# Up projections of two gated feed-forward layers by seven block products, with the normalised x as operand

## The chip, the cores and the metric

The kernel runs on one core of a Trainium2 chip. The metric is the device time of one execution in microseconds. Before the change three runs took 2679.86 to 2680.95 us, median 2680.18. The engines are TensorE (PE, with its weight loads shown apart as PEld), VectorE (DVE), ScalarE (ACT), GpSimd (POOL) and SyncE (SP), which here issues all the transfers.

## The reference, cut to what matters

A two-layer encoder works on 1024 prompt tokens and 32 tokens of a running stream, 1056 columns (TT) in all, with 1024 channels. Layer 0 has a gated convolution mixer, layer 1 an attention with a forget gate; each is followed by a feed-forward part:

```python
def _rmsnorm(x, g):
    y = xf * lax.rsqrt(jnp.mean(xf * xf, axis=-1, keepdims=True) + EPS)
    return (y * g)

def _conv_ffn(h, ctx, w_up, conv_w, w_down):       # h = _rmsnorm(x, ffn_norm[l])
    up = h @ w_up                                  # 1024 -> 2 * 2816
    upc, new_ctx = _causal_dwconv(up, ctx, conv_w) # three taps over time
    g, v = jnp.split(upc, 2, axis=-1)
    return (jax.nn.silu(g) * v) @ w_down, new_ctx  # 2816 -> 1024

x = x + f                                          # f is the result of _conv_ffn
```

All of it is float32.

## The kernel before

**Layout.** Channels lie in partitions, tokens along the free axis. x is eight tiles x[m] of 128 x 1056. Weights come as units of 128 x 1024: eight blocks of 128 x 128 (k = 0 to 7) that give one tile of 128 output channels.

**Precision.** Each operand is split into a rounded part (h, a copy by ACT) and the rest (l, a subtraction by DVE); a product is the three matmuls h*h, h*l and l*h (`chain`, L154 to L156). `weights` (L117) loads a unit, and splits it (L131, L132).

**An up unit** (`unit`, L170) has three column chunks of 352 (`CH`), with 8 x 3 matmuls each. Its operand is the split of the raw x times the norm's gain (`normed`, `split`). The factor 1/rms of each token, `rs`, is multiplied in when DVE reads the result from PSUM (L189). The first two units of a phase (`fresh`) don't wait for it: ACT copies them out as they are, and `settle` multiplies them later.

**The norm.** While x[m] is completed by the last down projection, ACT squares it and POOL (for the last m DVE) adds the square to acc (`square_add`, L205 and L206). `rstd` (L208) sums acc over partitions by a matmul with ones (L217), then works on tiles of 128 x 352 that hold the same number in all partitions: square root, reciprocal, one correcting step (L218 to L223).

**The feed-forward part** (`ffn`, L362). For each of 22 tiles t there are two units, g from unit t and v from unit 22 + t. Each goes through `halo`, `tail` (POOL copies of four columns) and `conv` (one ACT and two DVE instructions over 1058 columns, L266 to L268), g then through silu (L381); v*g (L383) is split into acth and actl (L140, L141). `pipeline` collects acts in groups of 2, 4, 4, 4, 4, 4. When the next group has its first act, `down` multiplies a group's acts by its w_down tiles: for each m and chunk, 3 matmuls per act, then DVE adds the PSUM bank to x[m] in SBUF (L291). x stays in SBUF through the whole part.

**The end.** The last group of layer 1 goes through `finish` (L226): four chunks of 264 columns (`ENDS`), each with its eight m, the sum of squares, the final norm, and the output's transfer. The last group of layer 0 calls `done(m)` for each m: x[m] is split for the attention (gain is folded into weights there) and spilled to DRAM. The attention phase reads x back for its output projection.

**Order.** The code is written for a scheduler that gives every instruction its engine's queue position and all semaphores at build time. Instructions written earlier have priority; one whose inputs or buffers aren't ready is passed by later ones. Engines then execute their queues in order. A pool of n buffers makes a writer wait until a buffer's last reader is done. PSUM has banks `d` (3 x 512), `s` (2 x 1024) and `o` (1 x 512) in all phases.

## Time and profile before

| what | value |
|---|---|
| median of three runs | 2680.18 us |
| the profiled execution: time; its span | 2678.83 us; 2677.0 us |
| mixer; feed-forward 0; attention; feed-forward 1 (stretches of the span, rounded) | 0 to 390; 390 to 1166; 1166 to 1890; 1890 to 2677 us |
| PE busy in 400 to 1166 (766 us) | 762.05 us |
| PE busy in 1890 to 2677 (787 us) | 766.28 us |
| bytes moved | 150.92 MB, mean 56 GB/s |

The span goes from the first to the last instruction; the time of an execution is 1.8 us longer here. A busy share is an average over stages, so stages are read from tables by stretch. PE's matmuls are pipelined: one is shown as some 320 ns long while the next starts after about half of that, so the pace is read from counts in a full stretch, not from the duration of one. In rows of groups the columns are: line, engine, operation, output<-inputs, shapes, count | busy us, mean ns of one | idle time of the engine before them and what ended it.

### The profile page before, as it was taken

What the parts mean: (1) busy time and instruction counts of PE and PEld (TensorE: products, weight loads), DVE (VectorE), ACT (ScalarE), POOL (GpSimd) and SP (SyncE); (2) the same over time, 40 slices, a digit from 0 to 9 for tenths busy, and PEclk for the clock granted to TensorE, in tenths of its full rate; (3) what the DMA queues carried; (4) which work ended last, traced back from release to release, by engine and by line L of the source; (5) the groups of instructions that cost most, each with busy time, mean ns of one, the idle gap of its engine ahead of it and who ended that gap; (6) DMA issues with size and microseconds to landing.
All of it is one profiled execution on the core that took longest, in us unless ns stands there. A gap on an engine that the chain in (4) does not pass through costs nothing.

```text
span 2677.0 us, 39027 instructions
## 1 busy us (share of the span) xinstructions
PE 2584.2 (97%) x16152; PEld 2534.1 (95%) x16152; DVE 1569.1 (59%) x2610; ACT 894.4 (33%) x1440; POOL 186.4 (7%) x291
## 2 busy tenths in 40 slices
PE   8999999999999999988999999999899999999997
PEld 7999999999999999988888888899899999999997
DVE  7444446554545455466787777767755454545547
ACT  4111133221212122235666656643422121212214
POOL 3000020000000000030000000001100000000003
PEclk9999999999999999989999999999999999999999
DMA  3111111111111111221221212261111111111111
GB/s 113 48 48 44 44 51 40 48 48 43 45 48 48 48 40 48 72 84 49 58 57 47 60 55 56 58 219 57 42 40 48 48 40 48 48 48 42 46 62 68
DMA packets 64929, 150.92 MB, mean 56 GB/s; under 512 B 12528, under 2 KB 34544, under 8 KB 64752
## 3 DMA queue, kind: packets, MB, share of 16 engines
q1 hardware_dynamic: 64752, 148.43, 17.1%
q8 instruction: 127, 2.08, 0.3%
q14 instruction: 50, 0.41, 0.0%
HBM read 121.87 MB, written 26.53 MB: 55 GB/s over the span
## 4 chain that ended last, share of the span: by engine, by line
PE 86%; DVE 8%; ACT 3%; issue 2%; DMA 1%; SPq 0%; DVEq 0%; ACTq 0%; POOL 0%; POOLq 0%
PE pb_d L154 15%; PE pb_d L155 15%; PE pb_d L156 15%; PE pb_s L154 8%; PE pb_s L156 8%; PE pb_s L155 8%; PE pb_o L154 4%; PE pb_o L156 4%; PE pb_o L155 4%; PE pb_o L624 2%; PE pb_d L635 1%; DVE pt L639 1%; DVE prob L580 1%; DVE wl L132 1%; DVE xl L144 1%
## 5 line engine op out<-in xcount | busy, mean ns | idle before, releaser
L154 PE MATMUL pb_d<-xh,wh 128*128 128x352 f32 (+2 forms) x1920 | 629.0, 329 | 16.9 <-ACT xh L143 7.1
L155 PE MATMUL pb_d<-xl,wh 128*128 128x352 f32 (+2 forms) x1920 | 627.6, 327 | 7.2 <-DVE xl L144 7.2
L156 PE MATMUL pb_d<-xh,wl 128*128 128x352 f32 (+2 forms) x1920 | 625.9, 326 | 1.1 <-DVE wl L132 0.9
L131 ACT ACTIVATE wh<-wraw 128x1024 fp32r<-128x1024 f32 (+1 forms) x197 | 208.1, 1056 | 1044.3 <-PE pb_d L155 445.8
L154 PEld LDWEIGHTS pb_d<-xh,wh 128*128 128x128 f32 x1920 | 364.8, 190 | 22.3 <-DVE pt L639 7.5
L155 PEld LDWEIGHTS pb_d<-xl,wh 128*128 128x128 f32 x1920 | 366.4, 191 | 9.8 <-DVE xl L144 9.4
L156 PEld LDWEIGHTS pb_d<-xh,wl 128*128 128x128 f32 x1920 | 365.5, 190 | 2.7 <-DVE wl L132 2.4
L132 DVE TENSOR_TENSOR wl<-wraw,wh 128x1024 fp32r<-128x1024 f32 (+1 forms) x197 | 244.9, 1243 | 102.6 <-ACT wh L131 102.2
L154 PE MATMUL pb_s<-xh,wh 128*128 128x352 f32 x896 | 292.2, 326 | 4.7 <-DVE u L189 4.7
L156 PE MATMUL pb_s<-xh,wl 128*128 128x352 f32 x896 | 290.0, 324 | 0.7 <-DVE wl L132 0.7
L155 PE MATMUL pb_s<-xl,wh 128*128 128x352 f32 x896 | 289.5, 323 | 0.0
L154 PE MATMUL pb_d<-acth,wh 128*128 128x352 f32 (+1 forms) x640 | 204.3, 320 | 0.8 <-ACT acth L140 0.8
L155 PE MATMUL pb_d<-actl,wh 128*128 128x352 f32 (+1 forms) x640 | 204.2, 319 | 0.4 <-DVE actl L141 0.4
L156 PE MATMUL pb_d<-acth,wl 128*128 128x352 f32 (+1 forms) x640 | 204.2, 319 | 0.0
L291 DVE TENSOR_TENSOR x<-x,pb_d 128x352 f32<-128x352 f32 x216 | 111.3, 519 | 155.7 <-PE pb_d L156 153.8
L189 DVE TENSOR_TENSOR u<-pb_d,rstd 128x352 f32<-128x352 f32 (+2 forms) x180 | 73.1, 429 | 210.3 <-PE pb_d L156 210.2
L154 PEld LDWEIGHTS pb_s<-xh,wh 128*128 128x128 f32 x896 | 169.1, 189 | 5.1 <-issue 4.9
L156 PEld LDWEIGHTS pb_s<-xh,wl 128*128 128x128 f32 x896 | 169.2, 189 | 1.0 <-DVE wl L132 1.0
L155 PEld LDWEIGHTS pb_s<-xl,wh 128*128 128x128 f32 x896 | 169.9, 190 | 0.2
L154 PE MATMUL pb_o<-xh,wh 128*128 128x352 f32 x448 | 145.2, 324 | 0.0
L156 PE MATMUL pb_o<-xh,wl 128*128 128x352 f32 x448 | 144.6, 323 | 0.0
L155 PE MATMUL pb_o<-xl,wh 128*128 128x352 f32 x448 | 144.3, 322 | 0.0
(237 smaller groups left out, 4729.5 us busy)
## 6 DMA issues: line engine op xcount, KB each, us to landing
wraw<-in_w_up SPq DMA_DIRECT2D x88, 512.0 KB
wraw<-in_w_down SPq DMA_DIRECT2D x44, 512.0 KB
wraw<-in_w_in SPq DMA_DIRECT2D x23, 512.0 KB
wraw<-in_w_kq SPq DMA_DIRECT2D x16, 512.0 KB
xd<-x SPq DMA_DIRECT2D x8, 528.0 KB
x<-xd SPq DMA_DIRECT2D x8, 528.0 KB
out_o_y<-y SPq DMA_DIRECT2D x16, 264.0 KB
wraw<-in_w_out SPq DMA_DIRECT2D x8, 512.0 KB
```

The costliest lines, as they stand in the source:

```text
L131: nc.scalar.activation(h[:, i:j], raw[:, i:j], AF.Copy)
L132: nc.vector.tensor_sub(l[:, i:j], raw[:, i:j], h[:, i:j].bitcast(F32))
L144: nc.vector.scalar_tensor_tensor(l[:, d], src[:, p], gain, h[:, d].bitcast(F32), op0=OP.mult, op1=OP.subtract)
L154: nc.tensor.matmul(ps, wh, xh[:, c[0]:c[1]], start=(i == 0), stop=False)
L155: nc.tensor.matmul(ps, wh, xl[:, c[0]:c[1]], start=False, stop=False)
L156: nc.tensor.matmul(ps, wl, xh[:, c[0]:c[1]], start=False, stop=(i == n - 1))
L189: nc.vector.tensor_mul(dst[:, d], ps[:, p.start - c[0]:p.stop - c[0]], self.rs[:, p])
L291: nc.vector.tensor_add(x[m][:, c[0]:c[1]], x[m][:, c[0]:c[1]], ps[:, :c[1] - c[0]])
L580: nc.vector.tensor_tensor_reduce(prob, ps, self.mask[:rows, end - w:end], -1.0, -NEG, OP.add, OP.min, st[:rows, i:i + 1])
L624: nc.tensor.matmul(ob[:, 256 - m:], vt[:, kt], pt[:, h * 512 + off:h * 512 + off + m], start=(kt == 0 and h == 0), stop=(kt == 2 * j + 1 a ...
L635: nc.tensor.transpose(ps[:, n:n + 128], probs[q][:, kt * 128:(kt + 1) * 128], self.ident)
L639: nc.vector.tensor_sub(pt[:, 512:512 + n], ps[:, :n], pt[:, :n].bitcast(F32))
```

## The change

**Seven products instead of eight.** Take the up projection for a pair of output tiles (g: "top" unit t, v: "low" unit 22 + t), the 1024 inputs in two halves of four blocks, and the tokens in two halves of 528 (`HALVES`). That is a 2 x 2 block product with eight block products. The change uses a form of Strassen's method with seven (`pair`): operands a11, s2, a12, s3, s1, a22 and a second s2 on the weights' side, where s1, s2, s3 are sums of blocks made by POOL; b11, t2, b21, t3, t1, t4, b22 on x's side. Each is split anew (`operand` for a block of 128 x 512). `product` runs one: two column halves of 264, four blocks, three matmuls. Partial results pass through `mid` and the two outputs u and v; two products accumulate in the bank of an earlier one.

**x normalised before.** The sums on x's side need the finished h. `begin` therefore multiplies x by gain and `rs` in place (DVE), splits it into b11, b12, b21, b22, runs the first pair of units on these without block products, and builds t1 to t4 from f1 to f4 (three sums on DVE, one on POOL, four splits, for each k). The first two units no longer start from raw x.

**x in DRAM.** x is now overwritten, so it is spilled first (`spill`: three pieces of 128 x 352 per m). Acts go down in groups of two (`stream`): for each m and chunk a piece of x is loaded, the PSUM bank added (DVE), and the piece stored again; 24 steps for a group, spread between the products of the next two pairs. Before the last group x is loaded whole (`load`), and `finish` or `down` get two acts instead of four.

**The norm with tokens in partitions.** `rstd` sums acc with 88 tokens as output partitions (one column per 88 tokens), does the short steps on 88 x n numbers, and spreads the result by a diagonal matrix (`diag`) and a matmul with ones. acc of the last m is made chunk by chunk (`late_square`).

**Buffers.** PSUM pools belong to a phase; the feed-forward phases have `d` (2 x 512) and `p` (3 x 1024). Four buffers hold split weights ("w"), five raw blocks ("wr"), three sums ("ws"), five pieces of x ("xs").

The core of the diff:

```diff
     def rstd(self, acc, cuts=CH):
...
+            ps = self.dbank()[:SIDE, :n]
+            for i in range(n):
+                a = c[0] + i * SIDE
+                nc.tensor.matmul(ps[:, i:i + 1], acc[:, a:a + SIDE], self.ones[:, :1], start=True, stop=True)
+            e, w, r = (self.sm.tile([SIDE, n], F32, name="n" + k, tag="n" + k, bufs=2) for k in "ewr")
+            nc.scalar.activation(e, ps, AF.Sqrt, bias=self.epst[:SIDE], scale=1.0 / D)
+            nc.vector.tensor_scalar(w, ps, -0.5 / D, -0.5 * EPS, op0=OP.mult, op1=OP.add)
+            nc.vector.reciprocal(r, e)
+            nc.vector.tensor_mul(e, r, r)
+            nc.vector.tensor_mul(e, e, w)
+            nc.vector.scalar_tensor_tensor(r, e, 1.5, r, op0=OP.add, op1=OP.mult)
+            dg = self.diag([SIDE, n, SIDE])
+            nc.vector.tensor_mul(dg, self.ident[:SIDE, None, :SIDE].to_broadcast([SIDE, n, SIDE]),
+                                 r[:, :, None].to_broadcast([SIDE, n, SIDE]))
             ps = self.dbank()[:, :c[1] - c[0]]
+            nc.tensor.matmul(ps, self.ones[:SIDE], dg.rearrange("p n c -> p (n c)"), start=True, stop=True)
+            nc.scalar.activation(out[:, cs], ps, AF.Copy)
             yield out[:, cs], c
...
+    def begin(self, x, acc, gain, units):
...
+        for i, c in enumerate(HALVES):
+            cs = slice(*c)
+            if i == 0:
+                next(norm), next(norm)
+            ps = [self.bank("p").rearrange("p (q c) -> p q c", q=2) for _ in units]
+            for m in range(NK):
+                nc.vector.scalar_tensor_tensor(x[m][:, cs], x[m][:, cs], self.gain[:, gain, m:m + 1], self.rs[:, cs],
+                                               op0=OP.mult, op1=OP.mult)
+                if i == 0 and m in (2, 4):
+                    next(norm)
+                n = "21"[m < k2] + "12"[i]
+                t = b[n][m % k2] = parts(x[m][:, cs], room(n != "12"))
+                for p, (h, l) in zip(ps, ws):
...
+        for k in range(k2):
+            b11, b12 = (x[k][:, slice(*c)] for c in HALVES)
+            b21, b22 = (x[k + k2][:, slice(*c)] for c in HALVES)
+            f = [self.slot("f", [128, 2, HB]) for _ in range(2)]
+            f1, f2, f3, f4 = f[0][:, 0], f[0][:, 1], f[1][:, 0], f[1][:, 1]
+            nc.vector.tensor_sub(f1, b12, b11)
+            nc.vector.tensor_sub(f2, b22, f1)
+            nc.gpsimd.tensor_sub(f4, f2, b21)
+            nc.vector.tensor_sub(f3, b22, b12)
+            for n, v in (("t2", f2), ("t3", f3), ("t1", f1), ("t4", f4)):
+                b[n][k] = parts(v, room(k == 0 or n in ("t1", "t2")))
+        return b, us
...
+    def operand(self, src):
+
+        nc = self.nc
+        t = self.wp.tile([128, 2, NK // 2, 128], F32R, name="wb", tag="w")
+        nc.scalar.activation(t[:, 0], src, AF.Copy)
+        nc.vector.tensor_sub(t[:, 1], src, t[:, 0].bitcast(F32))
+        return t
+
+    def product(self, ps, w, b, begin=True, end=True):
+
+        nc = self.nc
+        for q in range(2):
+            cs = slice(q * QB, (q + 1) * QB)
+            for k, t in enumerate(b):
+                for n, (i, j) in enumerate(((0, 0), (0, 1), (1, 0))):
+                    nc.tensor.matmul(ps[:, q, :QB], w[:, i, k], t[:, j, cs], start=(begin and k == 0 and n == 0),
+                                     stop=(end and k == len(b) - 1 and n == 2), skip_group_check=True)
+
+    def pair(self, top, low, b, us):
...
+        m, c11, u3 = two(mid), two(u[:, PAD:PAD + HB]), two(v[:, PAD:PAD + HB])
+        ps, p = bank()
+        self.product(ps, self.operand(a11), b["11"])
+        nc.scalar.activation(m, p, AF.Copy)
+        yield
+        nc.gpsimd.tensor_add(s1, a21, a22)
+        nc.gpsimd.tensor_sub(s2, s1, a11)
+        qs, q = bank()
+        self.product(qs, self.operand(s2), b["t2"])
+        nc.vector.tensor_add(m, m, q)
+        yield
+        self.product(ps, self.operand(a12), b["21"], begin=False)
+        nc.scalar.activation(c11, p, AF.Copy)
+        yield
+        nc.gpsimd.tensor_sub(s3, a11, a21)
+        qs, q = bank()
+        self.product(qs, self.operand(s3), b["t3"])
+        nc.vector.tensor_add(u3, m, q)
+        yield
+        rs, r = bank()
+        self.product(rs, self.operand(s1), b["t1"])
+        self.late(v, u3, r)
+        yield
+        qs, q = bank()
+        self.product(qs, self.operand(a22), b["t4"])
+        nc.vector.tensor_sub(u3, u3, q)
+        yield
+        nc.gpsimd.tensor_sub(s2, a12, s2)
+        self.product(rs, self.operand(s2), b["22"], begin=False)
+        self.late(u, m, r)
+        yield
...
+    def late(self, dst, src, ps):
+
+        for d, q, s in self.cuts():
+            self.nc.vector.tensor_add(dst[:, d], src[:, q, s], ps[:, q, s])
...
+    def stream(self, units, acts):
+
+        nc, g = self.nc, len(acts)
+        for m in range(NK):
+            if m * g % 4 == 0:
+                w = self.operand(self.block(units[m * g // 8], m * g // 4 % 2))
+            i = m * g % 4
+            for c, d in zip(CH, self.xd[m]):
+                t = self.slot("xs", [128, c[1] - c[0]], F32, "xs", 5)
+                nc.sync.dma_start(t, d)
+                ps = self.bank("d")[:, :c[1] - c[0]]
+                self.chain(ps, [(w[:, 0, i + k], w[:, 1, i + k]) for k in range(g)], acts, c)
+                nc.vector.tensor_add(t, t, ps)
+                nc.sync.dma_start(d, t)
+                yield
```

In `ffn` the loop over t = 1 to 21 runs `pair` and, after each product, as many steps of `stream` as are due: two for each product from the third on, one in the last two pairs, and what is left after the last pair.

## The prediction, made before the run

> **What bounds the kernel now.** First the page's span, busy times and chain of waits:

> ```profile
> span 2677.0 us, 39027 instructions
> PE 2584.2 (97%) x16152; PEld 2534.1 (95%) x16152; DVE 1569.1 (59%) x2610; ACT 894.4 (33%) x1440; POOL 186.4 (7%) x291
> PE 86%; DVE 8%; ACT 3%; issue 2%; DMA 1%; SPq 0%; DVEq 0%; ACTq 0%; POOL 0%; POOLq 0%
> q1 hardware_dynamic: 64752, 148.43, 17.1%
> ```

> TensorE sets the time. Busy shares average over stages, so next the table of busy times by stretch (from:to us, length, then PE, PEld, DVE, ACT, POOL busy and counts, granted clock, DMA share, GB/s):

> ```profile
> 500.00:1100.00 600.00, 600.00 (x3724) 600.00 (x3723) 304.36 (x416) 137.62 (x144) 11.66 (x76) 1.00 0.14 46
> 1300.00:1900.00 600.00, 564.45 (x3643) 531.41 (x3642) 444.89 (x957) 345.26 (x737) 52.75 (x33) 0.99 0.24 73
> 2631.00:2661.00 30.00, 30.00 (x246) 29.87 (x245) 25.83 (x54) 14.38 (x38) 13.23 (x17) 1.00 0.21 73
> ```

> The feed-forward stage (500 to 1100) never lets PE idle, at full clock: matmuls taken away there come off the time, if VectorE (DVE), at 51%, can carry what is added. Its 352-column matmuls start every 600/3724 = 161.1 ns. The last stretch has 264-column matmuls, the size that the change uses: 30/246 = 122.0 ns. So time follows the columns (ratio 0.757 for 0.75).

> The stops of PE at the seams (start, length, instruction, idle before it) and one clock row:

> ```profile
> 442.04 0.63 PE L154 MATMUL pb_d<-xh,wh 128*128 128x352 f32 x1 [3.95 <-DVE u L189]
> 442.47 0.49 PE L155 MATMUL pb_d<-xl,wh 128*128 128x352 f32 x1
> 1194.04 0.66 PE L550 MATMUL pb_d<-ident,raw 128*128 128x128 f32 x2 [8.78 <-issue]
> 1876.78 0.43 PE L154 MATMUL pb_d<-act,wh 128*128 128x352 f32 x1 [1.20 <-DVE x L291]
> 1890.03 0.43 PE L155 MATMUL pb_d<-xl,wh 128*128 128x352 f32 x1 [2.24 <-DVE xl L144]
> 1935.88 0.63 PE L154 MATMUL pb_s<-xh,wh 128*128 128x352 f32 x1 [4.67 <-DVE u L189]
> 441.00:452.00 11.00, 9.96 (x48) 9.99 (x49) 9.76 (x15) 4.37 (x4) 1.51 (x4) 0.73 0.13 50
> ```

> **A. The products: -113 us.** A pair of up units is now 2 x 3 x 8 x 3 = 144 matmuls of 352 columns, 23.2 us; it becomes 7 products x 2 halves x 4 blocks x 3 = 168 of 264, 20.5 us. 2.7 us x 21 pairs x 2 layers = 113. The first pair of a layer, unblocked, has 192 of 264: +0.2. Bounds: -122 (pure columns) to -105 (2% more per matmul). The down projections keep their 72 matmuls per act, 11.6 us; a pair with its act falls from 34.8 to 32.1.

> **B. What hides beside them: +10 us.** Rows that price DVE's and POOL's work (by form: count, busy, mean ns; the line of wl by source: min/median/max ns):

> ```profile
> L291 DVE TENSOR_TENSOR x<-x,pb_d 128x352 f32<-128x352 f32 x216 | 111.3, 519 | 155.7 <-PE pb_d L156 153.8 <-DMA wraw<-in_w_o 1.4
> L639 DVE TENSOR_TENSOR pt<-pb_d,pt 128x512 fp32r<-128x512 f32 x96 | 64.8, 685 | 57.6 <-ACT pt L638 57.2
> L268 DVE SCALAR_TENSOR_TENSOR y<-u,cv,y 128x1058 f32<-128x1058 f32 x96 | 126.6, 1320 | 2.7
> L383 DVE TENSOR_TENSOR y<-y 128x1058 f32<-128x1058 f32 x44 | 55.5, 1260 | 1.5
> L141 DVE TENSOR_TENSOR actl<-y,acth 128x1024 fp32r<-128x1024 f32 x52 | 63.7, 1224 | 40.9 <-ACT acth L140 40.9
> 2619.84 0.43 DVE L239 TENSOR_TENSOR x<-x,pb_d 128x264 f32<-128x264 f32 x1 [0.50 <-PE pb_d L156]
> L206 POOL TENSOR_TENSOR acc<-acc,sq 128x1056 f32<-128x1056 f32 x24 | 75.5, 3148 | 327.3 <-ACT sq L205 326.6
> L132 DVE TENSOR_TENSOR wl<-wraw,wh x197: 425/1225/3492, 5.3 to 2613.1; 128x1024 fp32r<-128x1024 f32 x195, 128x256 fp32r<-128x256 f32 x1, 128x768 fp32r<-128x768 f32 x1
> 1879.05 9.80 POOL L206 TENSOR_TENSOR acc<-acc,sq 128x1056 f32<-128x1056 f32 x3 [3.88 <-ACT sq L205]
> 1883.49 3.07 DVE L132 TENSOR_TENSOR wl<-wraw,wh 128x1024 fp32r<-128x1024 f32 x1
> ```

> DVE per pair and act: nine operand splits of 512 (seven blocks, two for down) at 0.69 = 6.2; three reads of a product (528) at 0.70 = 2.1; two late writes in pieces of 264, 232, 32 = 2.0; four convolution steps 5.3; gate 1.3; act split 1.4; twelve stream adds 6.2, twice as many as now, since groups go from four acts to two. Sum 24.5 of 32.1 us, 76%. (The same count for before gives 18.2 of 34.8, 52%, against the row's 51%.)

> ScalarE gets nine copies of 512, two PSUM reads and the act's work, some 12 of 32 us; it hides. POOL gets four block sums of 512: 3148 x 512/1056 = 1.53 us each, 6.1 per pair. They disturb: the split at 1883.49 took 3.07 us beneath a POOL sum, 1.22 usually, so DVE runs at 40% on instructions with two SBUF inputs; reads of PSUM do not stretch. Such instructions are 58% of the 24.5 us, so 6.1 x 0.6 x 0.58 = 2.1 us are lost: 26.6 of 32.1, 83%.

> [...]

> At 86% DVE the 2631 row has PE full; at 74% the attention row has it at 94%, with tight chains. I take the first and 0.25 us per pair: +10. Bounds 0 to +113 (all of A).

> Transfers: 1.5 MB of weights and 24 pieces of 180 KB per pair, 5.8 MB in 32 us, 182 GB/s. The queue row gives 148.43 MB in 17.1% of 2677 us, 324 GB/s while busy: 56%. Landing and issue:

> ```profile
> 2.13 3.62 DMA wraw<-in_w_in
> L122 SPq DMA_DIRECT2D wraw<-in_w_up x88: 327/328/333, 368.9 to 2532.8; - x88
> ```

> Thirty issues of 0.33 us (24 of the stream, six of weights) leave SP free. SP works in order: a store waits there for its add, and the weight blocks and loads behind it wait too. A stream step comes every 2.7 us; five buffers give 13 us for load, add and store, about 8 at 3.6 per landing. Hidden; if a piece is late, the add waits at the head of DVE, and the splits behind it keep PE waiting.

> **C. The start of each up projection: +44 us.** Today the raw x goes into the first two units and the norm is applied to their output, so the norm's chain stops PE only at 442 and 1936. After, nothing starts before the norm:
> - last sums to acc, the tiny matmuls, square root, five short operations, diagonal, matmul, copy. Today's chain, from 2664.3 to y's first step, is the nearest row:

> ```profile
> 2664.26 0.71 PE L217 MATMUL pb_o<-acc,ones 128*128 128x264 f32 x2 [2.76 <-DVE acc L206]
> 2665.87 1.79 DVE L220 RECIPROCAL rstd<-step 128x264 f32<-128x264 f32 x1
> 2669.09 3.48 DVE L248 SCALAR_TENSOR_TENSOR y<-x,gain,rstd 128x264 f32<-128x264 f32 x6
> ```

>   4.8 us; the reciprocal goes, two hand-offs come: 4. With scaling 0.73 and ACT's copy 0.63 PE idles about 6. In layer 1 the sum of squares is late too: x comes every 2.9 us, POOL adds one in 3.3 (9.80/3): +4.
> - the body: 16 scalings and splits, 16 x 1.43 = 22.9, and the rest of the norm 2 on DVE, against 192 x 0.122 = 23.4 on PE: +2.
> - the four sums: per k three on DVE and four splits, 28 x 0.70 = 19.6, and four sums on POOL of 1.58 that cost DVE 3.8. t2, the second product's input, is whole after 21 of these 23.4 us. PE has only the products of b11 and b21 to do, 5.9, and ends its units 2 later than DVE: +13.
> - the clock after two stops, 5 together; DVE's backlog of the first act (8 us) ahead of the first pair's reads, 3.

> 29 and 33 us. What goes: 3.95 + 3.0 in layer 0; 1.20 + 2.24 + 4.67 + 3.0 in layer 1. Net 22 + 22. Bounds: +20 (sums hidden under the body) to +70 (PE in written order, clock low throughout).

> [...]

> **D. Layer 0's end and attention's start: -3 us.** The last down has two acts, 2.9 us of PE per m, where POOL needs 3.1 and DVE 1.6 + 1.25 to 3.1; the same form at 1857 to 1890 cost 3.4 of stops: +5. The norm without three wide reciprocals shortens the 8.78 us stop: -8. Bounds -12 to +8.

> **E. The end: +8 us.** finish has half its PE work (23.4 us), but DVE's stays: 25.83 of 30 us in the 2631 row, 10.1 per chunk of 11.7, less 2.3 for the reciprocal and its steps: 7.8 against PE's 5.9, +8 over four chunks, less about 4 of stops that were there, and +4 for x, whose last pieces are read back only after the stream's last store, while the first chunk needs all eight x. Bounds 0 to +15.

> **Sum** against the profiled execution (2678.8 us, span 2677.0; the median of the runs is 1.4 above): -113 + 10 + 44 - 3 + 8 = -54, so 2625 us.

> **The rivals.** (1) Slower: POOL's block sums block DVE, which becomes the bound of each pair. For: 30.6 of 32.1 us at a full block, and order fixed beforehand. Against: full PE at 86% in the 2631 row. Price: all of A at 2.7 us per pair, 2625 - 10 + 113 = 2728; it turns slower from 54/42 + 0.25 = 1.5 us per pair. The same in part, 0.8 to 1.4 us: 2648 to 2673.
> (2) The starts are hidden better, C = +20 or less, and nothing stalls: 2625 - 24 - 10 = 2591. For: full PE from 500 to 1100. Against: DVE has no slack in the body.
> (3) No gain in the products, since loads of weights rise from 144 to 168 and set the pace, A = 0: 2625 + 113 = 2738. Against: 122.0 ns in the 2631 row, each with a load; 2 in 100.

> **Chances.** Forecast (2600 to 2648) 0.47; (2) 0.12; (1) in part 0.18; within 0.2% (5.4 us, what a measurement can tell from no change) 0.06; (1) in full and (3) 0.17. Range 2585 to 2690; the forecast's own 2600 to 2648. Faster 0.77, same 0.06, slower 0.17.

> **What would show it.** A: matmuls of 264 at 122 ns through the pairs. B: PE full and DVE near 83% there; rival 1: splits near 1.5 us beneath POOL's sums and PE waiting for wb or for adds. C: PE stops of about 6 and 13 us at each start, the second released by DVE's splits of t2. E: DVE over 95% in the last 45 us. Wrong if the pair's period is 34 us or more, or the starts cost under 15 us each.

## The result, and the profile after

Four runs of the changed kernel took 2773.91 to 2777.2 us, median 2775.97; four of the kernel before 2679.86 to 2680.95, median 2680.43. The ratio is 1.0356, with a 95% interval of 1.0338 to 1.0374: 96 us slower, where 55 us faster was forecast. It lies outside the range and above every rival.

The page of the changed kernel: span, busy times, queue and chain of waits.

```profile
span 2772.1 us, 45529 instructions
PE 2550.4 (92%) x17332; PEld 2471.8 (89%) x17332; DVE 1823.5 (66%) x3266; ACT 1057.2 (38%) x1850; POOL 473.7 (17%) x467
PE 14%; DMA 8%; DVE 3%; issue 1%; SPq 1%; POOL 0%; ACT 0%; DVEq 0%; POOLq 0%; ACTq 0%
q1 hardware_dynamic: 239568, 338.83, 40.9%
```

PE's busy share fell from 97 to 92%, and transfers, 1% of the chain before, are 8% of a chain that covers only part of the span. DVE, the forecast's worry, is at 66%. By stretch:

```profile
400.00:520.00 120.00, 89.34 (x622) 86.23 (x623) 93.17 (x145) 50.51 (x86) 35.24 (x28) 0.86 0.21 68
520.00:1120.00 600.00, 580.86 (x4268) 574.42 (x4267) 406.72 (x657) 193.25 (x284) 121.16 (x139) 0.99 0.58 174
2050.00:2650.00 600.00, 579.68 (x4274) 572.10 (x4273) 404.90 (x657) 193.32 (x284) 121.76 (x142) 1.00 0.59 174
2725.00:2772.00 47.00, 22.17 (x114) 20.02 (x113) 26.37 (x64) 17.51 (x48) 21.57 (x26) 0.66 0.26 93
```

A pair with its act is 168 + 72 = 240 matmuls, so the second row gives 240 x 600/4268 = 33.7 us per pair: less than the 34.8 of before, more than the forecast's 32.35. The first and last rows are worse: at the start of the feed-forward part PE is busy 89 of 120 us (116 of 120 before), and at the end 22 of 47 us, at a mean clock of 0.66.

The groups of instructions show what the steady stretches wait for, and the waits of SP's queue show where:

```profile
L173 PE MATMUL pb_d<-acth,wb 128*128 128x352 f32 (+1 forms) x992 | 331.6, 338 | 52.7 <-DVE xs L610 52.3
L610 DVE TENSOR_TENSOR xs<-xs,pb_d 128x352 f32<-128x352 f32 x480 | 246.9, 519 | 374.5 <-DMA xs<-xd 219.8 <-PE pb_d L175 133.2 <-PE pb_p L498 10.0
```

```profile
SPq L607 <- DMA xd<-xs: 719.7, 367, 4.8
```

PE's down matmuls wait for the stream's adds (L610), the adds 220 us for their loads, and the loads (L607) stand on SP 367 times for a store's landing, 719.7 us in all and 4.8 at most. What these waits hold up there is the subject of the first experiments.

To compare stages, I summed from the traces PE's idle time ahead of its instructions, plus half of PE's busy time at half clock (the traces of both kernels grant 1.0 or 0.5; us, idle + clock; "loads later" and "all orders" are runs below):

| stage | before | changed | loads later | all orders, second |
|---|---|---|---|---|
| mixer | 12.9 + 0 | 18.1 + 3.4 | 18.0 + 4.3 | 15.1 + 0 |
| start of up, layer 0 | 4.0 + 2.5 | 30.8 + 9.7 | 30.9 + 10.3 | 19.2 + 11.6 |
| pairs, layer 0 | 0 | 19.1 + 3.4 | 0 | 0 |
| end of layer 0 and attention's start | 15.2 + 5.4 | 25.8 + 14.0 | 23.8 + 12.3 | 26.6 + 9.5 |
| attention | 35.7 + 7.9 | 35.8 + 8.4 | 41.2 + 14.4 | 39.0 + 15.1 |
| start of up, layer 1 | 9.0 + 4.8 | 34.5 + 12.4 | 34.0 + 12.8 | 23.0 + 11.7 |
| pairs, layer 1 | 0 | 20.3 + 0 | 0 | 0 |
| end | 4.0 + 0 | 29.3 + 16.4 | 25.1 + 9.6 | 22.5 + 5.9 |
| sum | 101 | 281 | 237 | 199 |

After PE's last matmul the kernel goes on for 12.0 us before the change and 8.1 after it. The span less the sum and this tail is PE's work: 2564 us before, 2483 changed. The change does save 81 us of it, and loses 180 in stops and clock.

### The profile page after: what moved, and what is told of

The parts are those of the page before. It is cut to its first block, busy times and chain, and to the rows that moved or that the text cites. A ratio compares the mean times of both kernels' runs of the same rounds, so it can differ in the third digit from the quotient of the medians.

```text
span 2772.1 us, 45529 instructions
## 1 busy us (share of the span) xinstructions
PE 2550.4 (92%) x17332; PEld 2471.8 (89%) x17332; DVE 1823.5 (66%) x3266; ACT 1057.2 (38%) x1850; POOL 473.7 (17%) x467
## 3 DMA queue, kind: packets, MB, share of 16 engines
q1 hardware_dynamic: 239568, 338.83, 40.9%
## 5 line engine op out<-in xcount | busy, mean ns | idle before, releaser
L498 PE MATMUL pb_p<-b,wb 128*128 128x264 f32 x7056 | 951.1, 287 | 27.4 <-ACT u L530 14.8
L498 PEld LDWEIGHTS pb_p<-b,wb 128*128 128x128 f32 x7056 | 918.9, 190 | 31.8 <-ACT u L530 15.3
L610 DVE TENSOR_TENSOR xs<-xs,pb_d 128x352 f32<-128x352 f32 x480 | 246.9, 519 | 374.5 <-DMA xs<-xd 219.8
L173 PE MATMUL pb_d<-acth,wb 128*128 128x352 f32 (+1 forms) x992 | 331.6, 338 | 52.7 <-DVE xs L610 52.3
L175 PE MATMUL pb_d<-acth,wb 128*128 128x352 f32 (+1 forms) x992 | 326.3, 329 | 4.5 <-DVE wb L488 4.5
L174 PE MATMUL pb_d<-actl,wb 128*128 128x352 f32 (+1 forms) x992 | 324.9, 328 | 0.0
L173 PE MATMUL pb_d<-xh,wh 128*128 128x384 f32 (+2 forms) x864 | 287.4, 336 | 14.0 <-ACT xh L162 7.4
L174 PE MATMUL pb_d<-xl,wh 128*128 128x384 f32 (+2 forms) x864 | 285.6, 331 | 5.8 <-DVE xl L163 5.7
L175 PE MATMUL pb_d<-xh,wl 128*128 128x384 f32 (+2 forms) x864 | 284.8, 330 | 1.0 <-DVE wl L151 0.8
L173 PEld LDWEIGHTS pb_d<-acth,wb 128*128 128x128 f32 x992 | 190.4, 193 | 70.0 <-DVE xs L610 63.8
L175 PEld LDWEIGHTS pb_d<-acth,wb 128*128 128x128 f32 x992 | 191.9, 193 | 6.2 <-DVE wb L488 6.2
L174 PEld LDWEIGHTS pb_d<-xl,wh 128*128 128x128 f32 x864 | 166.7, 193 | 8.1 <-DVE xl L163 7.7
L859 DVE TENSOR_TENSOR pt<-pb_d,pt 128x512 fp32r<-128x512 f32 (+1 forms) x160 | 99.0, 632 | 60.4 <-ACT pt L858 59.3
```

The lines of the kernel that those rows point to most:

```text
L173: nc.tensor.matmul(ps, wh, xh[:, c[0]:c[1]], start=(i == 0), stop=False)
L174: nc.tensor.matmul(ps, wh, xl[:, c[0]:c[1]], start=False, stop=False)
L175: nc.tensor.matmul(ps, wl, xh[:, c[0]:c[1]], start=False, stop=(i == n - 1))
L498: nc.tensor.matmul(ps[:, q, :QB], w[:, i, k], t[:, j, cs], start=(begin and k == 0 and n == 0), stop=(end and k == len(b) - 1 and n == 2), ...
L610: nc.vector.tensor_add(t, t, ps)
L859: nc.vector.tensor_sub(pt[:, 512:512 + n], ps[:, :n], pt[:, :n].bitcast(F32))
```

## The experiments

**No transfers.** The stream without its loads and stores:

```diff
-                nc.sync.dma_start(t, d)
...
-                nc.vector.tensor_add(t, t, ps)
-                nc.sync.dma_start(d, t)
+                nc.vector.tensor_add(t, acts[0][0][:, c[0]:c[1]].bitcast(F32), ps)
```

> Leaves out x's round trip inside the groups: no load and no store of x around the adds of the down projection, and each add reads an activation tile in place of the old x. Instructions on PE, VectorE, ScalarE and GpSimd stay the same in number and size. Theory 1 (the transfers set the pace where the adds come close together: SP issues in order, loads wait there for landings, ready stores stand behind them): the stops of PE from 482 to 1126 us (19.1 us) and from 2050 to 2654 us (20.3) go, and so does most of the drains' loss at 1126-1180 and 2654-2772 us, about 2700 to 2715 us in all. Rival (the stops come from PE's own order and from VectorE, and transfers only happen to end the waits last): 2755 to 2776 us. The stops at the two starts (about 30 us each) stay in both.

2693.87 us, 82 less than the changed kernel: the stops of the pairs go, and the time falls even below the theory's range. The transfers, which the forecast called hidden, cost this time.

**The loads later.** Order on SP alone:

```diff
+                with self.tc.issue_after(self.put_back[-3].ins) if len(self.put_back) > 2 else nullcontext():
+                    nc.sync.dma_start(t, d)
...
+                self.put_back.append(nc.sync.dma_start(d, t))
```

> Only the order on SP changes: each load of x is put behind the store of three steps earlier, so that no store that is ready stands behind a load which waits for a landing. Bytes, buffers (five) and all other engines' work are as in the changed kernel. Theory 1a (order of SP's queue is the cause): the loads keep a lead of two or more over the adds, the stops of PE in the steady stretches fall from about 40 us to below 10, and the time falls to 2710 to 2735 us. Rival 1b (five buffers are too few for a load, an add and a store at landings of 2 to 4 us, whatever the order): 2765 to 2785 us, with the adds still waiting for loads.

2707.77 us, 68 less, ratio to before 1.0104 (1.0089 to 1.012): just below the theory's range. SP's queue in the changed kernel (start, length, instruction):

```profile
598.02 0.32 SPq L607 DMA_DIRECT2D xs<-xd  x1
598.43 0.38 SPq L611 DMA_DIRECT2D xd<-xs  x1
600.90 0.32 SPq L607 DMA_DIRECT2D xs<-xd  x1
601.33 0.38 SPq L480 DMA_DIRECT2D wr<-in_w_up  x1
601.75 0.42 SPq L611 DMA_DIRECT2D xd<-xs  x1
```

Some of the adds of the same time on DVE, with their idle time ahead (the first is that of step 34):

```profile
589.34 0.52 DVE L610 TENSOR_TENSOR xs<-xs,pb_d 128x352 f32<-128x352 f32 x1 [0.35 <-issue]
597.02 0.52 DVE L610 TENSOR_TENSOR xs<-xs,pb_d 128x352 f32<-128x352 f32 x1
600.49 0.52 DVE L610 TENSOR_TENSOR xs<-xs,pb_d 128x352 f32<-128x352 f32 x1 [1.94 <-DMA xs<-xd]
603.31 0.52 DVE L610 TENSOR_TENSOR xs<-xs,pb_d 128x352 f32<-128x352 f32 x1 [2.30 <-DMA xs<-xd]
607.36 0.52 DVE L610 TENSOR_TENSOR xs<-xs,pb_d 128x352 f32<-128x352 f32 x1 [2.31 <-DMA xs<-xd]
```

Counted along the trace, the store at 598.43 is that of step 34, whose add had ended at 589.86; in these 8.6 us three more adds ran, and the store stood behind loads on SP. The load at 600.90 (step 39) needs that same buffer, waits 2.5 us for the store's landing, and its add comes 2.4 us later. Finished pieces fill the buffers, and a load that has only just been issued is what the next add waits for: the adds come 3.4 us apart (597.02 to 607.36 in three steps), where 2.7 were wanted. With the order changed, loads are two to three adds ahead, and in the windows PE is full:

```profile
500.00:1100.00 600.00, 600.00 (x4500) 600.00 (x4499) 437.08 (x693) 207.66 (x302) 142.26 (x152) 1.00 0.60 183
2010.00:2610.00 600.00, 600.00 (x4498) 600.00 (x4497) 438.20 (x696) 206.88 (x300) 142.79 (x152) 1.00 0.60 184
```

240 x 600/4500 = 32.0 us per pair. (33.7 - 32.0) x 42 pairs = 71 us, about what the run gained (68). Bytes, buffers and DVE's work were the same, at even 9 GB/s more; so neither the rate nor the number of buffers was the cause.

The run without transfers is still 14 us lower. Behind the last pair of each layer the stream's remaining steps follow each other without products between; there PE waits 7.9 and 7.2 us for the stream's adds in this run, and 2.4 and 3.0 us in the run without transfers.

**Eight products, on the stream as it was and with the loads later.** The pair's body is replaced, and the sums leave `begin`:

```diff
+        for dst, blocks in ((u, (a11, a12)), (v, (a21, a22))):
+            o = [self.operand(z) for z in blocks]
+            for i in range(2):
+                ps, p = bank()
+                self.product(ps, o[0], b["1" + "12"[i]], end=False)
+                yield
+                self.product(ps, o[1], b["2" + "12"[i]], begin=False)
```

> Undoes the seven products alone: plain eight block products on the normalised operand, no sums of operand blocks on GpSimd, none of the sums of products on VectorE; x in DRAM between groups, the new norm and the stream stay. 42 products more at 24 matmuls x 122.0 ns are +123 us if PE were full both ways. Theory (the seven products' gain is there, and x in DRAM, the norm and the starts take more than it): the longer pairs cover part of the stream's stops (some 20 to 40 us), and the start is free of GpSimd's sums (10 to 20 us), so 2840 to 2880 us, 160 to 200 above the kernel before. Rival (the sums and splits of the seven products eat their gain): 2690 to 2790 us.

> Eight plain products in every pair, without the sums of operand blocks and of products, on the stream with the loads later: against 2707.8 us this is the price of the seven products alone. PE work is 42 products x 2.95 us = 124 us more. Theory (the start's sums and stops give back about 20 to 25 us per layer): 2770 to 2785 us, as with the stream unmended, where pairs had no stops. Rival 1 (the seven products' gain arrives in full): 2825 to 2835 us. Rival 2 (the stream's order held the eight products up too): 2740 to 2760 us.

2779.76 and 2782.21 us. The first fell to its rival in number: the seven products on the old stream gained nothing net. The second gives their price with the stream mended: 74 us. By stretch it has

```profile
500.00:1100.00 600.00, 600.00 (x4527) 600.00 (x4526) 301.53 (x432) 178.29 (x325) 10.50 (x68) 1.00 0.56 171
```

and 264 matmuls per pair and act, 35.0 us against 32.0: 3.0 x 42 = 126 us of PE. So about 50 are given back elsewhere: 28 by the sums at the start (the next runs), the rest was not traced. The old order of SP did not hurt eight products (their windows are full as well).

**No sums at the start**, on both streams; t1 to t4 are plain blocks, so that their 16 splits go with the sums (the first expectation says that all splits stay; they don't):

```diff
-        for k in range(k2):
...
+        b.update(t1=b["12"], t2=b["21"], t3=b["22"], t4=b["12"])
```

> Leaves out the four sums of operand blocks that GpSimd builds at each start (the products take plain blocks in their place, so the result differs); all products and splits stay. Theory (a start loses to VectorE's order, all eight scalings ahead of the splits, and to the norm's chunks in PE's queue; GpSimd beside VectorE slows them as a part): the stop of 7.05 us at 417.7 us shrinks by 2 to 4 us, units finish some 5 us earlier, in all 10 to 20 us off 2776: 2756 to 2766 us. Rival (the sums of operand blocks are themselves what the start waits for): the starts lose 20 us each less, 2730 to 2740 us.

> Stands on the run with the loads later (2707.8 us). Leaves out the four sums of operand blocks at each start; the products take plain blocks, so the result differs. Theory (the sums are the greater part of what a start costs: stops of 5.2 and 7.4 us after the first units, and late units): 10 to 15 us per layer, 2678 to 2690 us. Rival (the norm and the scalings ahead of them are, and the convolution of the first act comes late anyway): 2698 to 2706 us.

2719.57 us on the old stream, and 2679.26 with the loads later. The first fell below both ranges. Half of its 56 us were the stream's, which happened to break down less (in 520 to 1120 us it ran 4404 matmuls in place of 4268): the second, where the pairs have no stops with or without sums, says that the sums and their splits cost 28.5 us, 14 per layer. Stops of PE with the loads later, with sums (start, length, idle ahead):

```profile
419.96 0.59 PE L396 MATMUL pb_p<-b,wh 128*128 128x264 f32 x1 [7.05 <-DVE b L376]
457.90 9.33 PE L499 MATMUL pb_p<-b,wb 128*128 128x264 f32 x62 [1.82 <-DVE wb L489]
484.48 0.81 PE L499 MATMUL pb_p<-b,wb 128*128 128x264 f32 x2 [7.43 <-ACT u L531]
```

Without sums no stop over 0.4 us follows the first units; the stop of 7.05 us stays.

**Three orders, each on the loads later.** The start: all of the norm first, and a scaling between splits.

```diff
-                next(norm), next(norm)
+                for _ in norm:
+                    pass
...
+                with self.tc.issue_after(low[-2].ins) if len(low) > 1 else nullcontext():
```

> Stands on the run with the loads later (2707.8 us). At each start of an up projection the norm's four chunks are all written ahead of the units (two of them stood behind unit matmuls in PE's queue), and each scaling is put behind the split two blocks earlier, in place of eight scalings ahead of the first split. No instruction is added or taken away. Theory (order alone makes the stops of 7.05 us at 420.0, of 3.45 us at 440.0 and VectorE's idle 3.83 and 3.67 us): 10 to 20 us less over both layers, 2688 to 2698 us. Rival (VectorE's and GpSimd's whole work at the start, some 40 us, sets it and order only moves the waits): 2702 to 2710 us.

2701.39 us, 6.4 less, between the two ranges and next to the rival's. The 7.05 us became 0.5, but a new stop stands behind it:

```profile
419.04 0.39 PE L397 MATMUL pb_p<-b,wh 128*128 128x264 f32 x1 [0.50 <-DVE b L376]
450.90 0.81 PE L500 MATMUL pb_p<-b,wb 128*128 128x264 f32 x2 [6.21 <-ACT wb L489]
479.38 1.03 PE L500 MATMUL pb_p<-b,wb 128*128 128x264 f32 x3 [6.81 <-ACT u L532]
```

The first pair by plain products, the sums beside it:

```diff
+            for i, _ in enumerate((self.plain_pair if t == 1 else self.pair)(...)):
+                if t == 1 and i % 2:
+                    sums(i // 2)
```

> Stands on the run with the loads later (2707.8 us). The first pair of each layer is computed by eight plain products, and the four sums of operand blocks are built beside them, for the second pair on. That is 24 matmuls x 122.0 ns = 2.9 us more PE work per layer. Theory (the sums at the start have nothing of PE beside them; the stops from 454 to 485 us, 5.2 and 7.4 us, and late units are their price, some 20 us per layer with the clock): 2672 to 2688 us. Rival (VectorE is behind anyway, and the sums only move into the first pair): 2700 to 2715 us.

2697.99 us, 9.8 less, between the two ranges: under half of the theory's least gain. Behind the first units PE is full to 476 us and then waits 2.98 us for a weight split and, at 499.8, 5.15 us for the first act. The finish's norm a chunk later:

```diff
+            if j:
+                out(ENDS[j - 1])
+        out(ENDS[-1])
```

> Stands on the run with the loads later (2707.8 us). Only the finish changes: the norm and the output of a chunk of tokens are written behind the next chunk's matmuls, so that the tiny norm matmuls do not wait in PE's queue ahead of work that is ready. Theory (order in PE's queue, with the clock at half after each stop, costs the finish some 15 us): 2690 to 2698 us. Rival (VectorE is full in the finish, as the forecast's term E has it): 2703 to 2710 us.

2704.31 us, 3.5 less: the rival's number, and no clear gain, since the runs of both overlap (2704.1 to 2712.3 and 2701.5 to 2708.5). But both steps of the norm still stood side by side. Apart:

```diff
+                if j and m == 2:
+                    next(norm)
+                if j and m == 6:
+                    out(ENDS[j - 1])
```

> Stands on the run with the loads later (2707.8 us). The finish alone: the two small matmul steps of a chunk's norm are written apart, the first behind the third and the second behind the seventh block of the next chunk's matmuls, so that neither waits in PE's queue for VectorE's short operations (in the run of the finish's order both still stood side by side, with stops of 3.4 to 4.1 us). Theory (PE's queue order sets the finish; VectorE is busy only 26.4 of the last 47 us in the changed kernel): PE's stops of 3.4 to 4.8 us per chunk fall below 1.5, 2690 to 2699 us. Rival (the chain of adds, squares and sums of x on VectorE and ScalarE per chunk sets it, whatever PE's order): 2701 to 2708 us.

2699.3 us, 8.5 less: 0.3 above the theory's range, and stops of more than 1.5 us remain. PE in the changed kernel's finish, then in this run's:

```profile
2735.13 1.04 PE L238 MATMUL pb_d<-ones,acc 128*88 128x1 f32 x6 [4.78 <-DVE acc L225]
2737.84 1.25 PE L250 MATMUL pb_d<-dg,ones 88*128 88x264 f32 x2 [1.67 <-DVE dg L247]
2747.80 1.04 PE L238 MATMUL pb_d<-ones,acc 128*88 128x1 f32 x6 [3.96 <-DVE acc L225]
```

```profile
2663.48 0.71 PE L253 MATMUL pb_d<-dg,ones 88*128 88x264 f32 x2 [1.57 <-DVE dg L250]
2672.84 1.22 PE L253 MATMUL pb_d<-dg,ones 88*128 88x264 f32 x2 [3.82 <-DVE dg L250]
2681.99 1.25 PE L253 MATMUL pb_d<-dg,ones 88*128 88x264 f32 x2 [1.58 <-DVE dg L250]
```

With the loads later, PE stood 17.8 us in all ahead of the norm's matmuls in the finish; with the steps apart it is 10.5. Queue order is a part of the end's price, then. What holds the rest, the chain of adds, squares and sums by the rival, was not tested.

**The norm alone**, in the kernel before (`rstd` and `diag` of the change, nothing else):

> The kernel before with one part of the change alone: the norm with tokens in partitions; raw x still goes into the first units, eight products, x stays in SBUF. Theory (the norm costs the mixer some 10 us, since its second small matmul stands in PE's queue and waits for VectorE while ready unit matmuls stand behind it: 4.13 us of stop at 46.1 us, 3.4 of clock; at the start of attention it gains what the wide reciprocals cost, some 4 to 8 us): 2680 to 2692 us, with attention starting within 6 us of before. Rival (the norm is cheap everywhere but in the mixer's profile by chance): 2668 to 2678 us, faster than before.

2695.73 us, ratio 1.0062 (1.0047 to 1.0077): 16 us slower, and above the theory's range. The first wait for the scores before, then rows with the norm:

```profile
1229.77 0.77 PE L600 MATMUL pb_s<-kb,qb 68*128 68x128 f32 x2 [5.89 <-DMA qb<-qbd]
```

```profile
46.15 1.51 PE L232 MATMUL pb_d<-dg,ones 88*128 88x352 f32 x2 [4.08 <-DVE dg L229]
1199.17 1.54 PE L232 MATMUL pb_d<-dg,ones 88*128 88x352 f32 x2 [0.93 <-DVE dg L229]
1239.51 0.77 PE L613 MATMUL pb_s<-kb,qb 68*128 68x128 f32 x2 [5.42 <-DMA qb<-qbd]
```

In the mixer the second small matmul waits in PE's queue with ready unit matmuls behind it. At attention's start the stop of 8.78 us (1194.04 in the prediction's rows) is gone, replaced by four of 0.5 to 1.1 us, and yet the first scores come 9.7 us later than before, where the theory allowed 6. DVE's splits of x show why: they start 9.2 us later than before at the end of the mixer and 12.0 later at the end of layer 0, so the shorter stop won back only 2.3 us. The attention then takes 6 us more (the last section).

**All orders together**, with the old norm in the mixer (first edit); then also the first stream of a layer later and loads four steps behind:

```diff
+        norm, self.settled = self.rstd if self.settled else self.wide_rstd, True
...
-                fill, acts, n, at = self.stream(a["w_down"][l, t - 2:t], acts), [], 3 * NK, -2
+                fill, acts, n, at = self.stream(a["w_down"][l, t - 2:t], acts), [], 3 * NK, -5 if t == 2 else -2
...
-                while n and (3 * NK - n) * (12 if t < NF - 2 else 24) < at * 3 * NK:
+                while n and (3 * NK - n) * (9 if t < 4 else 12 if t < NF - 2 else 24) < at * 3 * NK:
...
-                with self.tc.issue_after(self.put_back[-3].ins) if len(self.put_back) > 2 else nullcontext():
+                with self.tc.issue_after(self.put_back[-4].ins) if len(self.put_back) > 3 else nullcontext():
```

> All orders together: loads later, the norm ahead of the units and scalings between splits at the start, the first pair by plain products with the sums beside them, the finish's norm a chunk later, and the old wide norm in the mixer alone. If the gains of the single runs add (6.4, 9.8, 3.5) and the mixer gives back 10 us: 2707.8 - 29.7 = 2678 us, 2672 to 2684, no different from before. Rival (the same backlog of VectorE and ScalarE at the start stands behind each of them, so that each gain is counted twice): 2685 to 2697 us.

> The run of all orders with two numbers changed: each load of x stands behind the store four steps earlier (three before), and the first stream of a layer begins three products later and goes at 24 steps in nine products (twelve before). Theory (in the drain of a stream a step of 0.97 us needs load and store of 2.3 to 2.5 us each within five buffers, so a load issued one step earlier takes away some 3 us per layer; the stop of 5.15 us at 499.8 us, where the first stream waits for the first acts, goes): 12 to 16 us less than the run of all orders, 2660 to 2670 us. Rival (the act chain is late by the backlog and the stop moves to the stream's end): within 4 us of it.

Ten runs each: 2675.95 us, ratio to before 0.9982 (0.9971 to 0.9994), as the sum of the single gains had it; and 2671.35 us, 0.9978 (0.9965 to 0.9990). Both beat the kernel before, by some 0.2%. The second lies 4.6 us below the first, not 12 to 16, and the runs of both overlap (2666.5 to 2681.1 and 2668.3 to 2683.7). The stop of 5.17 us behind the first acts, at 484.0 in the first, did not go, it moved (PE in the second):

```profile
487.17 0.95 PE L175 MATMUL pb_d<-acth,wb 128*128 128x352 f32 x2 [7.45 <-ACT acth L620]
```

Then, on the second, the finish's norm apart as above; and on top of that the first stream eight products late:

```diff
-                fill, acts, n, at = self.stream(a["w_down"][l, t - 2:t], acts), [], 3 * NK, -5 if t == 2 else -2
+                fill, acts, n, at = self.stream(a["w_down"][l, t - 2:t], acts), [], 3 * NK, -8 if t == 2 else -2
...
-                while n and (3 * NK - n) * (9 if t < 4 else 12 if t < NF - 2 else 24) < at * 3 * NK:
+                while n and (3 * NK - n) * (6 if t < 4 else 12 if t < NF - 2 else 24) < at * 3 * NK:
```

> The second run of all orders (2671.4 us) with the finish's norm in two steps apart. Theory (queue order): 6 to 12 us less, 2659 to 2666 us. Rival (chain on VectorE and ScalarE): within 3 us of it.

> As the run before it in this list, with the first stream of a layer eight products late (five before) at 24 steps in six products. Theory (the stop of 7.4 us at 487 us waits for the first two acts, which VectorE and ScalarE end then whatever PE does; the stream's first down matmul comes later than that): the stop goes in both layers, 8 to 14 us less than it, 2648 to 2658 us. Rival (three products more ahead of the acts load VectorE with their reads and sums, and the acts end as much later): within 4 us of it.

2675.09 and 2678.74 us, 0.998 (0.9969 to 0.9992) and 0.9997 (0.9988 to 1.0006). Neither helps; single runs of one kernel lie up to 15 us apart here, so the finish's 4 us the other way say little. In the last, the first stream comes eight products later and PE stops for 7.07 us at 487.5 all the same, now for a copy of `u` on ACT. In all four runs of all orders PE waits 5 to 7.5 us between 479 and 488 us for work that ACT ends, whatever stands there in its queue.

## Why the prediction was wrong, step by step

The terms, changed kernel less before (products and B by pair periods from the windows, the rest from the table of stages):

| term | forecast | changed | loads later |
|---|---|---|---|
| A products | -113 | -117 | -117 |
| B beside them | +10 | +71 | 0 |
| mixer | 0 | +9 | +9 |
| C starts | +44 | +67 | +68 |
| D end of layer 0, attention's start | -3 | +19 | +15 |
| attention | 0 | +1 | +12 |
| E end | +8 | +42 | +31 |
| unassigned | | +3 | +15 |
| span | -54 | +95 | +33 |

What is unassigned holds +7 us for the norm's own small matmuls (PE's work in the run with the norm alone is that much above the kernel before) and -4 for the shorter tail. That closes the sum of the changed kernel; with the loads later 12 us stay open. In the table of stages B shows 43 of its 71 us as stops and clock; the other 28 lie in PE's busy time, so that PE's work falls by 81 us there and not by A's 117 (the norm's matmuls add the 7).

- **A was right**: 32.0 us per pair where nothing stops, against 32.1, from the 122.0 ns of one row. The rival without any gain is out.
- **B failed at one sentence**: "five buffers give 13 us for load, add and store, about 8 at 3.6 per landing. Hidden". The landings were even shorter (2.4 and 2.5 us in the rows above), and the rate was right (182 GB/s worked out, 183 measured). But it counted a store as starting when its add ends; that of step 34 was issued 8.6 us later. The prediction had even written that SP works in order and that a store waits there for its add; it did not ask the reverse, what stands behind a load that waits for a buffer. That is the next store, and through it the next buffer. The cost was 71 us in place of nothing. The prediction's own sign, a period of 34 us or more, was just missed at 33.7. The 10 us that it did count for DVE's chains are not there: with the order mended B is 0.
- **Rival 1 was wrong**, in size and not in mechanism: DVE is busy 437 of 600 us in full pairs, 73%, not 83%. POOL's sums do hold up DVE's splits (run with the loads later, DVE, then POOL):

```profile
468.00 1.63 DVE L376 TENSOR_TENSOR b<-f,b 128x528 fp32r<-128x528 f32 x1
469.55 1.79 DVE L376 TENSOR_TENSOR b<-f,b 128x528 fp32r<-128x528 f32 x1
471.26 0.70 DVE L376 TENSOR_TENSOR b<-f,b 128x528 fp32r<-128x528 f32 x1
```

```profile
467.43 1.62 POOL L411 TENSOR_TENSOR f<-f,x 128x528 f32<-128x528 f32 x1 [1.33 <-DVE f L410]
469.02 1.76 POOL L525 TENSOR_TENSOR ws<-ws,wr 128x512 f32<-128x512 f32 x1
```

The sums end at 469.05 and 470.78, and the split that started beneath each ends some 0.57 us later; the third split, beside no sum, takes 0.70. In all of this run, 80 DVE instructions of 512 or 528 columns that read SBUF alone started beneath a POOL sum: 69 ended 0.55 to 0.57 us after the sum's end, and the other 11 took their usual 0.7, beneath three sums that took 2.9 to 4.8 us in place of some 1.3 to 1.8. So one waited for the other's end here; DVE does not run at 40% of its pace, as the prediction read the 3.07 us at 1883.49 (that split, too, ended 1.08 us after the sum over it, which ends at 1885.48 in the trace). But this doesn't cost DVE the sums' whole time, as rival 1 counts by the author's estimate (24.5 + 6.1 = 30.6 us): 25 of DVE's 692 instructions in the full window from 500 us are held up, for 17.6 us, 0.9 per pair, where the forecast had 2.1 and the rival 6.1, and in the pairs PE is full through it.
- **C was 67 us for 44**, near its upper bound of 70. Right were the first stop (6 us forecast, 2.66 + 1.75 + 1.22) and the sums with their splits: 13 forecast, 14 measured. Wrong was "the body ... +2": DVE does all eight scalings in a row (8.56 us in place of 8 x 0.73, beneath POOL) ahead of the first splits, and two of the norm's chunks stand in PE's queue behind unit matmuls; those stops are 7.05, 1.23 and 3.46 us. The clock takes 10 to 12 us per start, not 5. Nor was it order alone: DVE is busy 70.8 of the 90 us from 400, PE 59.3, and when order took the stop of 7.05 us away, one of 6.21 us came 31 us later.
- **The mixer was left out.** The norm's new form went to it too. There a matmul that waits for DVE inside a queue of ready ones cost 4.1 us, and the clock behind it 3.4.
- **D and E** left out the stream's drain, the steps that remain behind a layer's last pair with no products between them: PE waits there for the stream's adds 9.4 us in layer 0 and 12.4 at the end. At the end, the other 16.9 us of stops stand ahead of the norm's matmuls. The norm of each chunk went from one matmul and wide operations to two steps on PE with a chain of short operations between, in the order of PE's queue, and with half the PE work per chunk there is little to cover it; the low clock (0.66 in the last row of windows, tail included) adds 16 us. DVE was to be over 95% busy at the end and is busy 26.4 of 47 us, so its load alone was not the limit. In layer 0's last down, waits for DVE's adds to x take 6.5 us (+5 forecast); at attention's start the norm and what hangs on it stop PE for 3.9 us in place of 8.8 (-8 forecast).

The sign came out wrong because five terms were each too low: B by 61 us, E by 34, C by 23, D by 22 and the mixer by 9. B alone would have brought the sum to +7, about no change. In B, the mixer and a part of C and E, order on a queue had been counted as free; no rival joined these terms.

## What to carry to other kernels

On a queue that works in order, list for each wait what stands behind it and whether that frees what the waiter needs: a load that waits for a buffer must not stand ahead of the store that empties one (the other order took 68 us off here). Before PE work is cut by a quarter, count the other engines' work in the stages where it is new (here a start with 22.9 + 19.6 us of DVE's by the forecast's own count, beside 23.4 + 5.9 of PE): moving one stop there mostly showed the next. A cheaper form of a helper (the norm) must be priced at each place that calls it.

## What the runs showed of the hardware

The attention's instructions are the same in all these kernels, and its work moved nowhere. Still this stretch, from the first to the last of its transposing matmuls, differs. Before, and then in the first run of all orders (columns as in the windows above):

```profile
1233.00:1852.00 619.00, 583.29 (x3771) 546.21 (x3770) 455.95 (x1035) 364.56 (x806) 40.33 (x32) 0.99 0.24 73
```

```profile
1226.00:1858.00 632.00, 591.02 (x3771) 553.12 (x3770) 456.45 (x1035) 364.02 (x806) 40.24 (x32) 0.97 0.25 71
```

It took 619 us in the changed kernel too, and 622 to 633 in all runs but these two, with 4 to 9 stretches of low clock that begin in it in place of 4 (of 3.41 us each, at 0.5, before and in the changed kernel). The longest stop in this stretch of the second row's run is the one below, 3.28 us; in the second run of all orders it is 1.72 us, with 8 stretches of low clock, and before it is 1.72 us too, with 4. So a longer stop doesn't account for that run's further ones. What does stays open; it takes up to 13 us from each mended version.

```profile
1786.21 0.66 PE L175 MATMUL pb_d<-act,wh 128*128 128x352 f32 x1 [3.28 <-DVE x L347]
```
